# A two-layer diffusion step on one core: three quarters of a modulation vector move from TensorE to VectorE, and the table that spreads VectorE's dot products is given other shares

## The chip, the core and the metric

The kernel runs on one core of a Trainium2 chip. The metric is device time in microseconds (us): the median of three runs before is 2429.84 us (2428.86 to 2434.89). One further execution was profiled. Its parts are named as the profile names them: PE is TensorE's matmul row, PEld its weight loads, DVE is VectorE, ACT is ScalarE, POOL is GpSimd, SP is SyncE, which issues nearly all loads. "L415" is line 415 of the kernel before.

## The reference, cut to what matters

Two layers of a trunk are applied to 128 context tokens and 128 latent tokens of width 2048. The context tokens are modulated by `c_ctx`, the latent ones by `c`; otherwise they share all weights.

```
m = silu(cond) @ w_mod[l] + b_mod[l]          # cond: c_ctx, and c; six vectors of 2048
shift1, scale1, gate1, shift2, scale2, gate2 = split(m, 6)
q_r, k_r, v_r, g_r, q_a, k_a, v_a = split((rms(x) * (1 + scale1) + shift1) @ w_in[l])
x = x + gate1 * (concat(retention(...), attention(...)) @ w_out[l])
h = (rms(x) * (1 + scale2) + shift2) @ w_up[l]
x = x + gate2 * ((silu(gate) * val of a width-3 conv of h) @ w_down[l])
```

The six modulation vectors of a layer have the numbers 0 to 5 in this order. Vector 2, `gate1`, is the one that scales the output projection before it is added to `x`. All matrices are fp32 in memory; every weight is read once, 611.64 MB in all.

## The kernel before, in words

**The matmuls.** All tokens stand in the free dimension (256 columns). A big weight is cut into 128x128 tiles, and eight of them make a *piece* (512 KB, one DMA). There are 768 pieces in a fixed order: of layer 0 the heads (kv, q, ret; pieces 0 to 87), the output projection (88 to 119), then up and down projections in three thirds (120 to 383); of layer 1 kv and q (384 to 407), ret (408 to 471), out (472 to 503), up and down (504 to 767). Each weight is split into a rounded part `hi` (by ACT, L482) and the rest `lo` (by DVE, L483), and a tile takes three matmuls of 256 columns, hi by hi, hi by lo and lo by hi (L674 to L676). The splits run `LOOK` = 3 pieces ahead of PE: four pairs of buffers.

**The side tasks.** Attention and retention of a head are generators (`q_task`, `ret_task`); each piece ends with one step of the oldest one (a second step in mid-piece when two wait), so their small matmuls (L825 to L987, into PSUM tiles `aux`) stand between pieces, and their DVE and ACT parts stand in those engines' queues in the order of emission. No engine reorders its queue.

**The modulation vectors** are made in two ways. On PE: `emit_mod` and `emit_modq` multiply 32 columns of the condition by 128x512 tiles of `w_mod` (L406, L392); `emit_modq` makes a quarter of a vector (512 outputs) from four loads of 1 MB with four matmuls each, and `close_mod` copies the result on ACT, transposes it on PE (L447, four times) and reduces it on DVE. On DVE: `emit_dot` multiplies a row block of 128 outputs of `w_mod` by the broadcast condition and sums along the row (L415); a unit is one load of 1 MB and two such dot products, one for each condition. `DVESEQ` lists the vectors made this way, `PESEQ` and `QSEQ` those made on PE.

**Where they stand.** Before anything is emitted, `body` writes a list of events. PE's events follow `quota`, a line through the `knots`, in pairs: two loads' worth of matmuls after a piece. DVE's dot products follow `plan`: each has a due piece (six before the first use of its vector); `room` says how many dot products a piece may take in relation to others, from `DSHARE` by the kind of the piece, a fixed number in the heads of layer 0, and none from 6 pieces before to 12 behind the start of a norm (`QNORM`). A credit that grows with `room` times the rate still needed places them, mostly in twos on neighbouring pieces.

**The loads.** `pump` issues on SP's queue, in the order of the events, loads of modulation weights into `MODB` = 3 buffers `vec` and loads of pieces into `RAWB` = 5 buffers `raw`. A `vec` load is issued when the third-last user has released its buffer; SP waits at it, and what stands behind it in SP's queue waits too.

Of the kernel before, what the change touches and what calls it, by code (L numbers as in the profile page):

```python
# [48 lines left out]
def build_work():  # L49
# [51 lines left out]
    for it in items:  # L101
        g = groups[it["g"]]
        key = g["key"]
        for a in range(0, len(it["order"]), PIECE):
# [16 lines left out]
MU = KC * KC // MUNIT  # L121
# [2 lines left out]
PESEQ = [(0, 2), (0, 3)]  # L124

QSTART = [(0, 1 - i // 2, b) for b in range(4) for i in (0, 2)]
QMID = [(1, 2, 1), (1, 2, 2), (1, 2, 3)]
QNORM = {("up", 0): (0, 5, 0), ("kv", 1): (1, 2, 0), ("up", 1): (1, 5, 0)}
QSEQ = QSTART + QMID + list(QNORM.values())
DVESEQ = [(l, v, u) for l, v, n in ((0, 4, 0), (0, 5, 4), (1, 1, 0), (1, 0, 0), (1, 4, 0), (1, 3, 0), (1, 5, 4))  # L130
          for u in range(n, KC)]
DSHARE = {"kv": 0.38, "q": 0.38, "ret": 0.38, "out": 0.42, "up": 0.36, "down": 0.42}


@with_exitstack
def body(ctx: ExitStack, tc: tile.TileContext, io):
# [5 lines left out]
    mods = [("mod", (l, v, u)) for l, v in PESEQ for u in range(MU)]  # L142
    mods += [("modq", (*q, h)) for q in QMID for h in range(MU // 4)]
    dots = [(*d, k) for d in DVESEQ for k in range(2)]
    issued = [0, 0]
    gstart = {}
# [11 lines left out]
    def dot_event():  # L158

        if issued[1] < len(dots):  # L160
            l, v, u, k = dots[issued[1]]
            events.append(("dot", (l, v, u, k)))
            if (u, k) == (KC - 1, 1):
# [1 line left out]
            issued[1] += 1  # L165

    ahead = 3 * 2 * WIDE
    knots = [(ahead - 5, 0), (gstart["out", 0], 3 * MU // 2), (gstart["up", 0] - 6, 2 * MU), (gstart["kv", 1] + 16, 2 * MU),
             (gstart["out", 1] - 2, 11 * MU // 4)]

    def quota(j, knots):
        if j <= knots[0][0]:
# [9 lines left out]
    room = [0.0] * len(pieces)  # L182
    for j, p in enumerate(pieces):
        g = groups[p["it"]["g"]]
        ends = any(gstart[k] - 6 < j <= gstart[k] + 12 for k in QNORM)
        if not ends:
            if j >= gstart["out", 0]:
                room[j] = DSHARE[g["kind"]]
            elif j >= ahead or j >= 2 * WIDE and j % (2 * WIDE) >= 11:
                room[j] = 0.3  # L190
    plan, credit, nd = [0] * len(pieces), 0.0, 0
    for j in range(len(pieces)):
        while nd < len(dots) and due[nd] <= j:
# [25 lines left out]
    for j, p in enumerate(pieces):  # L219
        g = groups[p["it"]["g"]]  # L220
        kind, l = g["kind"], g["l"]
        if "gb" in p["it"] and p["first"]:
            w = 0 if kind == "kv" else 1
            start = j
            q = QNORM[kind, l]
# [20 lines left out]
        if j < 3 * nq:  # L246
            q, i = divmod(j, nq)
# [69 lines left out]
    def pump():  # L317

        while nload["mod"] < len(loads["mod"]) and held["mod"] < MODB:
# [3 lines left out]
            if key[0] == "dot":  # L323
                at = (DVESEQ.index(key[1]),)
            else:
# [94 lines left out]
    def end_dots(l, v):  # L420
        u = min(d[2] for d in DVESEQ if d[:2] == (l, v))
        dst = modT[l][:, v, u:, :]
        bias = C("bmod", l * 96 + v * KC + u, KC - u)
        nc.vector.tensor_tensor(dst, dst, bias.unsqueeze(2).to_broadcast([P, KC - u, 2]), op=ALU.add)
        if v in (1, 4):
            nc.vector.tensor_scalar_add(dst, dst, 1.0)
# [568 lines left out]
    with tc.manual_schedule():  # L995
# [13 lines left out]
        for ev, arg in events:  # L1009
# [31 lines left out]
            else:  # L1041
                j, hs = arg
# [12 lines left out]
def layout(inputs):  # L1055
# [21 lines left out]
    wm = a["w_mod"].reshape(DEPTH, D, 6, KC, P)  # L1077
    arrays["w_dot"] = np.stack([wm[l, :, v, u].T for l, v, u in DVESEQ])
    arrays["cb"] = np.ascontiguousarray(np.broadcast_to(np.stack([a["c_ctx"].reshape(D), a["c"].reshape(D)]), (P, 2, D)))
# [72 lines left out]
```

## Time and profile before

| | |
|---|---|
| median of three runs | 2429.84 us (2428.86 to 2434.89) |
| profiled execution: its own time, its span | 2432.38 us, 2430.6 us |
| PE busy, PEld busy | 2371.9 us (98%), 2204.5 us (91%) |
| DVE busy, ACT busy | 1892.6 us (78%), 1242.9 us (51%) |
| dot products on DVE (L415) | 208 of 2285 ns |
| splits on DVE (L483), on ACT (L482) | 768 of 1222 ns, 768 of 1051 ns |
| quarter matmuls on PE (L392), records | 448, of which 96 (three quarters) are touched |
| HBM read | 611.64 MB, 254 GB/s over the span |

A matmul's record is longer than the time to the next one, because they are pipelined; what one costs is read from start to start. The same holds, less so, for DVE. The 98% of PE is an average: it does not say how much of the span PE waits, which is read from the waits. The stretches of the program begin at these times in the trace: heads of layer 0 at 33.9 us, out at 388.7, up and down from 502.7, layer 1's kv and q at 1268.9, its ret pieces at 1343.6, its out at 1567.4, its up from 1669.3.

### The profile page before, as it was taken

What the parts mean: (1) busy time and instruction counts of PE and PEld (TensorE: products, weight loads), DVE (VectorE), ACT (ScalarE), POOL (GpSimd) and SP (SyncE); (2) the same over time, 40 slices, a digit from 0 to 9 for tenths busy, and PEclk for the clock granted to TensorE, in tenths of its full rate; (3) what the DMA queues carried; (4) which work ended last, traced back from release to release, by engine and by line L of the source; (5) the groups of instructions that cost most, each with busy time, mean ns of one, the idle gap of its engine ahead of it and who ended that gap; (6) DMA issues with size and microseconds to landing.
All of it is one profiled execution on the core that took longest, in us unless ns stands there. A gap on an engine that the chain in (4) does not pass through costs nothing.

```text
span 2430.6 us, 44608 instructions
## 1 busy us (share of the span) xinstructions
PE 2371.9 (98%) x18094; PEld 2204.5 (91%) x18094; DVE 1892.6 (78%) x2565; ACT 1242.9 (51%) x2005; POOL 27.5 (1%) x29
## 2 busy tenths in 40 slices
PE   6999999999999999999999999999999999999997
PEld 3888888899999999999989999999999888888886
DVE  4567777869998899889987787796997567666666
ACT  4534434465544555445556544456555555555555
POOL 0000010000000000000000000000000000000000
PEclk9999999999999999999999999999999999999999
DMA  9988788976787777777775687777675555655553
GB/s 382 351 310 325 277 301 321 354 261 240 282 283 272 252 275 254 275 271 252 264 281 192 245 290 280 289 275 257 231 245 188 190 186 182 190 190 186 190 181 122
DMA packets 146558, 619.27 MB, mean 255 GB/s; under 512 B 16304, under 2 KB 22448, under 8 KB 121392
## 3 DMA queue, kind: packets, MB, share of 16 engines
q1 hardware_dynamic: 138816, 605.24, 70.5%
q10 hardware_dynamic: 7536, 11.19, 1.3%
q8 instruction: 141, 2.31, 0.4%
q14 instruction: 65, 0.53, 0.1%
HBM read 611.64 MB, written 4.72 MB: 254 GB/s over the span
## 4 chain that ended last, share of the span: by engine, by line
PE 87%; DVE 6%; DMA 3%; issue 2%; ACT 2%; SPq 0%; DVEq 0%; POOLq 0%; ACTq 0%; POOL 0%
PE acc L674 20%; PE acc L676 19%; PE acc L675 19%; PE acc L614 15%; PE acc L616 8%; DVE lo L483 2%; PE md L392 2%; DVE hua L415 2%; DMA vec<-in_w_modq 1%; DMA vec<-in_w_mod 1%; PE md L406 1%; ACT hi L482 0%; ACT pr L874 0%; PE aux L902 0%; PE aux L447 0%
## 5 line engine op out<-in xcount | busy, mean ns | idle before, releaser
L483 DVE TENSOR_TENSOR lo<-raw,hi 128x1024 fp32r<-128x1024 f32 x768 | 934.4, 1222 | 245.2 <-ACT hi L482 241.3
L482 ACT CAST hi<-raw 128x1024 fp32r<-128x1024 f32 x768 | 804.0, 1051 | 476.7 <-PE acc L675 354.8
L674 PE MATMUL acc<-hT,hi 128*128 128x256 f32 x3328 | 950.5, 286 | 5.9 <-ACT hT L577 5.9
L676 PE MATMUL acc<-hT,lo 128*128 128x256 f32 x3328 | 931.3, 280 | 2.0 <-DVE lo L483 2.0
L675 PE MATMUL acc<-hT,hi 128*128 128x256 f32 x3328 | 931.8, 280 | 0.6 <-DVE hT L582 0.6
L674 PEld LDWEIGHTS acc<-hT,hi 128*128 128x128 f32 x3328 | 626.9, 188 | 35.4 <-issue 17.0
L675 PEld LDWEIGHTS acc<-hT,hi 128*128 128x128 f32 x3328 | 625.8, 188 | 4.5 <-issue 1.9
L676 PEld LDWEIGHTS acc<-hT,lo 128*128 128x128 f32 x3328 | 627.0, 188 | 3.0 <-DVE lo L483 2.8
L415 DVE SCALAR_TENSOR_TENSOR hua<-vec,cbc 128x2048 bf16<-128x2048 f32 x208 | 475.2, 2285 | 0.7 <-DMA vec<-in_w_dot 0.7
L676 PE MATMUL acc<-ypair,lo 128*128 128x256 f32 x1216 | 344.3, 283 | 2.3 <-DVE lo L483 2.3
L674 PE MATMUL acc<-ypair,hi 128*128 128x256 f32 x1216 | 346.0, 285 | 0.0
L675 PE MATMUL acc<-ypair,hi 128*128 128x256 f32 x1216 | 344.0, 283 | 0.0
L614 PE MATMUL acc<-hT,hi 128*128 128x512 f32 x896 | 316.7, 396 | 0.0
L616 PE MATMUL acc<-hT,lo 128*128 128x256 f32 x896 | 252.7, 282 | 0.0
L614 PE MATMUL acc<-ypair,hi 128*128 128x512 f32 x704 | 247.2, 396 | 0.0
L674 PEld LDWEIGHTS acc<-ypair,hi 128*128 128x128 f32 x1216 | 233.2, 192 | 6.8 <-issue 5.0
L676 PEld LDWEIGHTS acc<-ypair,lo 128*128 128x128 f32 x1216 | 233.2, 192 | 3.0 <-DVE lo L483 3.0
L675 PEld LDWEIGHTS acc<-ypair,hi 128*128 128x128 f32 x1216 | 233.3, 192 | 0.1
L614 PEld LDWEIGHTS acc<-hT,hi 128*128 128x128 f32 x896 | 168.4, 188 | 40.6
L616 PE MATMUL acc<-ypair,lo 128*128 128x256 f32 x704 | 197.5, 281 | 0.0
L616 PEld LDWEIGHTS acc<-hT,lo 128*128 128x128 f32 x896 | 168.3, 188 | 0.0
L614 PEld LDWEIGHTS acc<-ypair,hi 128*128 128x128 f32 x704 | 132.1, 188 | 31.5
(145 smaller groups left out, 1584.2 us busy)
## 6 DMA issues: line engine op xcount, KB each, us to landing
raw<-in_w_up SPq DMA_DIRECT2D x352, 512.0 KB, 4.4
vec<-in_w_dot SPq DMA_DIRECT2D x104, 1024.0 KB, 5.2
raw<-in_w_in SPq DMA_DIRECT2D x176, 512.0 KB, 5.4
raw<-in_w_down SPq DMA_DIRECT2D x176, 512.0 KB, 4.2
vec<-in_w_modq SPq DMA_DIRECT2D x56, 1024.0 KB, 7.2
vec<-in_w_mod SPq DMA_DIRECT2D x32, 1024.0 KB, 8.0
raw<-in_w_out SPq DMA_DIRECT2D x64, 512.0 KB, 5.5
xT<-in_xT ACTq DMA_DIRECT2D x2, 1024.0 KB, 9.9
```

Source lines behind the costliest of these rows:

```text
L392: nc.tensor.matmul(md[0][32 * j:32 * j + 32, :], sc[:, 2 * kc:2 * kc + 32], t[:, 512 * i:512 * i + 512], start=kc < 4, stop=kc >= 12)
L406: nc.tensor.matmul(md[0][32 * j:32 * j + 32, :], sc[:, 2 * u:2 * u + 32], t[:, 512 * j:512 * j + 512], start=u == 0, stop=u == MU - 1)
L415: nc.vector.scalar_tensor_tensor(hua.rearrange("p c t -> p (c t)").bitcast(BF16), raw[key], 1.0, acc[:, k, :], op0=ALU.mult, op1=ALU.mult, ...
L482: nc.scalar.copy(hi, r)
L483: nc.vector.tensor_tensor(lo, r, hi.bitcast(F32), op=ALU.subtract)
L614: nc.tensor.matmul(out, hi_t[j][:, P * i:P * i + P], src, start=c[n] == 1, stop=False, skip_group_check=True)
L616: nc.tensor.matmul(out[:, 0:256], lo_t[j][:, P * i:P * i + P], src[:, 0:256], start=False, stop=c[n] == nk, skip_group_check=True)
L674: nc.tensor.matmul(out, hi, src[:, 0:256], start=first, stop=False, skip_group_check=True)
L675: nc.tensor.matmul(out, hi, src[:, 256:512], start=False, stop=False, skip_group_check=True)
L676: nc.tensor.matmul(out, lo, src[:, 0:256], start=False, stop=last, skip_group_check=True)
```

## The change

`QMID` held quarters 1, 2 and 3 of layer 1's vector 2; they are taken from PE, and the 12 units of 128 outputs that they made are put into `DVESEQ` between vectors 0 and 4 of layer 1. Quarter 0 stays on PE, in the norm at the start of layer 1. The two knots that spread the PE events over layer 1's heads go. And `DSHARE` and the number for the heads of layer 0 are changed, which moves dot products of all vectors.

```
--- before.py
+++ after.py
@@ -124,12 +124,12 @@
 PESEQ = [(0, 2), (0, 3)]
 
 QSTART = [(0, 1 - i // 2, b) for b in range(4) for i in (0, 2)]
-QMID = [(1, 2, 1), (1, 2, 2), (1, 2, 3)]
+QMID = []
 QNORM = {("up", 0): (0, 5, 0), ("kv", 1): (1, 2, 0), ("up", 1): (1, 5, 0)}
 QSEQ = QSTART + QMID + list(QNORM.values())
-DVESEQ = [(l, v, u) for l, v, n in ((0, 4, 0), (0, 5, 4), (1, 1, 0), (1, 0, 0), (1, 4, 0), (1, 3, 0), (1, 5, 4))
+DVESEQ = [(l, v, u) for l, v, n in ((0, 4, 0), (0, 5, 4), (1, 1, 0), (1, 0, 0), (1, 2, 4), (1, 4, 0), (1, 3, 0), (1, 5, 4))
           for u in range(n, KC)]
-DSHARE = {"kv": 0.38, "q": 0.38, "ret": 0.38, "out": 0.42, "up": 0.36, "down": 0.42}
+DSHARE = {"kv": 0.5, "q": 0.5, "ret": 0.5, "out": 0.5, "up": 0.32, "down": 0.42}
 
 
 @with_exitstack
@@ -165,8 +165,7 @@
             issued[1] += 1
 
     ahead = 3 * 2 * WIDE
-    knots = [(ahead - 5, 0), (gstart["out", 0], 3 * MU // 2), (gstart["up", 0] - 6, 2 * MU), (gstart["kv", 1] + 16, 2 * MU),
-             (gstart["out", 1] - 2, 11 * MU // 4)]
+    knots = [(ahead - 5, 0), (gstart["out", 0], 3 * MU // 2), (gstart["up", 0] - 6, 2 * MU)]
 
     def quota(j, knots):
         if j <= knots[0][0]:
@@ -187,7 +186,7 @@
             if j >= gstart["out", 0]:
                 room[j] = DSHARE[g["kind"]]
             elif j >= ahead or j >= 2 * WIDE and j % (2 * WIDE) >= 11:
-                room[j] = 0.3
+                room[j] = 0.4
     plan, credit, nd = [0] * len(pieces), 0.0, 0
     for j in range(len(pieces)):
         while nd < len(dots) and due[nd] <= j:
```

With 232 dot products for 208 the plan comes out so (dot products by stretch, before and now; PE's pairs are where they were but for those taken out):

| pieces | before | now |
|---|---|---|
| 24 to 87, heads of layer 0 | 20 | 24 |
| 88 to 119, out of layer 0 | 14 | 18 |
| 120 to 183, first up | 24 | 20 |
| 184 to 383, the rest of layer 0 | 86 | 88 |
| 384 to 407, kv and q of layer 1 | 5 | 7 |
| 408 to 471, ret of layer 1 | 27 | 40 |
| 472 to 503, out of layer 1 | 14 | 17 |
| 504 to 567, up of layer 1 | 18 | 18 |

From line 169 on, a line of the changed kernel has a number lower by one. Three places follow.

DVE in the second attention task of layer 1, around pieces 412 to 416 (`lo` is the split of a piece, `hua` a dot product, `st` and `pr` are the softmax's, `modT` on L424 and L426 the bias of a finished vector), before:

```order
L483 TENSOR_TENSOR lo<-raw,hi 128x1024
L880 TENSOR_TENSOR st<-st 128x4
L881 RECIPROCAL st<-st 128x4
L882 TENSOR_TENSOR pr<-pr,st 128x512
L415 SCALAR_TENSOR_TENSOR hua,modT<-vec,cbc 128x2048
L424 TENSOR_TENSOR modT<-modT,cst 128x32
L426 TENSOR_SCALAR modT<-modT 128x32
L483 TENSOR_TENSOR lo<-raw,hi 128x1024
L880 TENSOR_TENSOR st<-st 128x2
L881 RECIPROCAL st<-st 128x2
L882 TENSOR_TENSOR pr<-pr,st 128x512
L483 TENSOR_TENSOR lo<-raw,hi 128x1024 x2
```

and now:

```order
L482 TENSOR_TENSOR lo<-raw,hi 128x1024
L879 TENSOR_TENSOR st<-st 128x4
L880 RECIPROCAL st<-st 128x4
L881 TENSOR_TENSOR pr<-pr,st 128x512
L414 SCALAR_TENSOR_TENSOR hua,modT<-vec,cbc 128x2048
L482 TENSOR_TENSOR lo<-raw,hi 128x1024
L879 TENSOR_TENSOR st<-st 128x2
L880 RECIPROCAL st<-st 128x2
L881 TENSOR_TENSOR pr<-pr,st 128x512
L414 SCALAR_TENSOR_TENSOR hua,modT<-vec,cbc 128x2048
L482 TENSOR_TENSOR lo<-raw,hi 128x1024 x2
L865 TENSOR_REDUCE st<-aux 128x2
```

A dot product stands now behind each of the two normalisations, where before the second had none behind it.

DVE in a retention task of layer 1, the head whose first step is at piece 440 (`bs`, `ag` and `grs` are the group norm's statistics, `ro` its result, `ry` and `ypair` the gated output), before:

```order
L975 BN_STATS bs<-ro 128x6 x2
L977 BN_AGGR ag<-bs 128x2 x2
L978 TENSOR_SCALAR grs<-ag 128x2
L483 TENSOR_TENSOR lo<-raw,hi 128x1024
L982 TENSOR_SCALAR ro<-ro,ag,grs 128x128 x2
L483 TENSOR_TENSOR lo<-raw,hi 128x1024
L989 SCALAR_TENSOR_TENSOR ry<-aux,cst,grp 128x256
L799 TENSOR_TENSOR ypair<-ry,ypair 128x256
L415 SCALAR_TENSOR_TENSOR hua,modT<-vec,cbc 128x2048
L483 TENSOR_TENSOR lo<-raw,hi 128x1024
L415 SCALAR_TENSOR_TENSOR hua,modT<-vec,cbc 128x2048
```

and now:

```order
L974 BN_STATS bs<-ro 128x6 x2
L976 BN_AGGR ag<-bs 128x2 x2
L977 TENSOR_SCALAR grs<-ag 128x2
L414 SCALAR_TENSOR_TENSOR hua,modT<-vec,cbc 128x2048
L482 TENSOR_TENSOR lo<-raw,hi 128x1024
L981 TENSOR_SCALAR ro<-ro,ag,grs 128x128 x2
L414 SCALAR_TENSOR_TENSOR hua,modT<-vec,cbc 128x2048
L482 TENSOR_TENSOR lo<-raw,hi 128x1024
L988 SCALAR_TENSOR_TENSOR ry<-aux,cst,grp 128x256
L798 TENSOR_TENSOR ypair<-ry,ypair 128x256
L482 TENSOR_TENSOR lo<-raw,hi 128x1024
L414 SCALAR_TENSOR_TENSOR hua,modT<-vec,cbc 128x2048
```

Where a head's eight pieces held two to four dot products, they hold five.

SP's queue in the output projection of layer 0, up to the load of the first part of the norm's quarter (`in_w_modq`), before:

```order
L329 DMA vec<-in_w_dot 128x2048
L329 DMA vec<-in_w_mod 128x2048 x2
L339 DMA raw<-in_w_out 128x1024 x4
L329 DMA vec<-in_w_dot 128x2048
L339 DMA raw<-in_w_out 128x1024 x3
L329 DMA vec<-in_w_dot 128x2048
L329 DMA vec<-in_w_mod 128x2048
L339 DMA raw<-in_w_out 128x1024
L329 DMA vec<-in_w_mod 128x2048
L339 DMA raw<-in_w_out 128x1024 x2
L339 DMA raw<-in_w_up 128x1024
L329 DMA vec<-in_w_modq 128x2048
```

and now:

```order
L328 DMA vec<-in_w_dot 128x2048 x2
L328 DMA vec<-in_w_mod 128x2048
L338 DMA raw<-in_w_out 128x1024 x4
L328 DMA vec<-in_w_mod 128x2048
L338 DMA raw<-in_w_out 128x1024 x3
L328 DMA vec<-in_w_dot 128x2048 x2
L328 DMA vec<-in_w_mod 128x2048
L338 DMA raw<-in_w_out 128x1024 x3
L328 DMA vec<-in_w_mod 128x2048
L338 DMA raw<-in_w_up 128x1024 x3
L328 DMA vec<-in_w_modq 128x2048 x3
```

The first load of the norm's quarter, which followed a dot product's release, now stands behind the second load of the last pair of `in_w_mod`, and is released by the first matmuls of that pair.

## Rows read from the trace of the kernel before

**Rows 1.** The page: busy time by engine, and the chain that ended last.

```profile
PE 2371.9 (98%) x18094; PEld 2204.5 (91%) x18094; DVE 1892.6 (78%) x2565; ACT 1242.9 (51%) x2005; POOL 27.5 (1%) x29
...
PE 87%; DVE 6%; DMA 3%; issue 2%; ACT 2%; SPq 0%; DVEq 0%; POOLq 0%; ACTq 0%; POOL 0%
```

**Rows 2.** Windows: stretch, us, busy of each engine, clock, DMA share, GB/s.

```profile
33.90:388.70 354.80, 338.59 (x2711) 292.89 (x2712) 243.97 (x399) 158.58 (x259) 8.66 (x7) 0.99 0.84 321
388.70:502.70 114.00, 111.56 (x915) 99.24 (x913) 87.88 (x111) 51.21 (x90) 1.38 (x2) 1.00 0.90 346
780.40:961.30 180.90, 180.90 (x1538) 180.90 (x1537) 167.73 (x209) 92.25 (x127) 0.00 (x0) 1.00 0.74 260
...
1440.00:1560.00 120.00, 119.45 (x996) 113.98 (x996) 93.86 (x138) 50.98 (x74) 7.26 (x5) 1.00 0.79 283
```

**Rows 3.** PE in order of time around a pair: start us, us, instruction.

```profile
1446.24 0.28 PE L676 MATMUL acc<-hT,lo 128*128 128x256 f32 x1
1446.45 1.92 PE L392 MATMUL md<-vec,sc 128*32 128x512 f32 x16
1448.30 0.39 PE L674 MATMUL acc<-hT,hi 128*128 128x256 f32 x1
1448.53 0.28 PE L675 MATMUL acc<-hT,hi 128*128 128x256 f32 x1
```

**Rows 4.** PE in order of time around a quarter's transposes.

```profile
1566.89 0.28 PE L676 MATMUL acc<-hT,lo 128*128 128x256 f32 x1
1567.02 0.60 PE L447 MATMUL aux<-cst,mev 128*128 128x128 f32 x4
1567.37 0.36 PE L674 MATMUL acc<-ypair,hi 128*128 128x256 f32 x1
```

**Rows 5.** DVE in order of time in a retention head of layer 1.

```profile
1463.96 2.28 DVE L415 SCALAR_TENSOR_TENSOR hua<-vec,cbc 128x2048 bf16<-128x2048 f32 x1
...
1466.17 1.22 DVE L483 TENSOR_TENSOR lo<-raw,hi 128x1024 fp32r<-128x1024 f32 x1
```

**Rows 6.** The same window's dot products (L415) alone: busy us, records.

```profile
1440.00:1560.00 120.00, 35.40 (x31) 1.00 0.79 283
```

**Rows 7.** Chain of waits in layer 1's second attention task: start, us, what.

```profile
1375.36 2.38 DVE lo L483 x2
1377.73 0.61 DVE st L866
...
1379.97 0.66 PE aux L889 x4
```

**Rows 8.** Chain of waits in out of layer 0, piece 101.

```profile
430.20 7.62 DMA vec<-in_w_mod
```

**Rows 9.** SP and PE at the norm's quarter of layer 0.

```profile
478.30 0.33 SPq L329 DMA_DIRECT2D vec<-in_w_modq  x1
478.51 1.92 PE L406 MATMUL md<-vec,sc 128*32 128x512 f32 x16
483.87 1.07 PE L392 MATMUL md<-vec,sc 128*32 128x512 f32 x8
```

**Rows 10.** Line L329, all loads of modulation weights.

```profile
DMA to landing us min/median/max: 4.7/6.4/14.0
```

**Rows 11.** Chain of waits in the heads of layer 0, piece 51.

```profile
211.13 0.57 DVE hua L415
...
215.36 10.16 DMA vec<-in_w_mod
```

**Rows 12.** PE's waits from 208.5 to 388.7 us: total, times, longest.

```profile
PE aux L968 <- DVE rk L954: 2.8, 3, 2.0
PE aux L889 <- ACT pr L874: 2.7, 3, 1.5
PE md L406 <- DMA vec<-in_w_mod: 2.4, 2, 1.6
```

**Rows 13.** PE's waits from 560 to 576 us, in the first up.

```profile
PE acc L676 <- DVE lo L483: 1.6, 2, 0.9
```

More of the change, by code (lines that the diff above doesn't have):

```diff
@@ L126 @@
 QSTART = [(0, 1 - i // 2, b) for b in range(4) for i in (0, 2)]
-QMID = [(1, 2, 1), (1, 2, 2), (1, 2, 3)]
+QMID = []
 QNORM = {("up", 0): (0, 5, 0), ("kv", 1): (1, 2, 0), ("up", 1): (1, 5, 0)}
 QSEQ = QSTART + QMID + list(QNORM.values())
-DVESEQ = [(l, v, u) for l, v, n in ((0, 4, 0), (0, 5, 4), (1, 1, 0), (1, 0, 0), (1, 4, 0), (1, 3, 0), (1, 5, 4))
+DVESEQ = [(l, v, u) for l, v, n in ((0, 4, 0), (0, 5, 4), (1, 1, 0), (1, 0, 0), (1, 2, 4), (1, 4, 0), (1, 3, 0), (1, 5, 4))
           for u in range(n, KC)]
-DSHARE = {"kv": 0.38, "q": 0.38, "ret": 0.38, "out": 0.42, "up": 0.36, "down": 0.42}
+DSHARE = {"kv": 0.5, "q": 0.5, "ret": 0.5, "out": 0.5, "up": 0.32, "down": 0.42}
 @with_exitstack
@@ L167, in body @@
     ahead = 3 * 2 * WIDE
-    knots = [(ahead - 5, 0), (gstart["out", 0], 3 * MU // 2), (gstart["up", 0] - 6, 2 * MU), (gstart["kv", 1] + 16, 2 * MU),
-             (gstart["out", 1] - 2, 11 * MU // 4)]
+    knots = [(ahead - 5, 0), (gstart["out", 0], 3 * MU // 2), (gstart["up", 0] - 6, 2 * MU)]
     def quota(j, knots):
@@ L189, in body @@
             elif j >= ahead or j >= 2 * WIDE and j % (2 * WIDE) >= 11:
-                room[j] = 0.3
+                room[j] = 0.4
     plan, credit, nd = [0] * len(pieces), 0.0, 0
```

## The prediction

> **What bounds the kernel now.** I read the page first. PE is busy 98% of the span, and the chain that ended last lies on PE for 87%, on DVE for 6% and on loads for 3% [rows 1]: work taken off PE shortens the span, unless another engine or a load is late where it was. DVE's 78% is a mean, so I read stretches next [rows 2]. In an up stretch of layer 0 DVE is busy 167.73 of 180.90 us (93%) and PE all of it, so 93% alone makes no wait there. In the heads of layer 0 PE is idle for 16.2 of 354.8 us, in the out projection of layer 0 for 2.4 of 114.0, in layer 1's ret pieces (window 1440 to 1560) for 0.6 of 120. Third, the chain and the waits inside the stretches, to see what ended PE's idle time: side tasks that pass through DVE, and loads into the three `vec` buffers [rows 7, 8, 11, 12]. The sum is made against the profiled execution, 2432.38 us; it stands 2.5 us above the median of 2429.84, and I carry the difference over unchanged.
>
> **1. PE's work that goes.** Six pairs of two loads (eight matmuls each) and three closings. From the matmul before a pair to the one behind it are 1448.30 − 1446.24 = 2.06 us [rows 3], where an ordinary step is 1567.02 − 1566.89 = 0.13 [rows 4], 0.12 as a mean of neighbouring ones; and the matmul behind the pair is 0.23 from the next instead of 0.12. A pair thus costs 2.06 − 0.12 + 0.11 = 2.05, six cost 12.3. A closing's four transposes cost 1567.37 − 1566.89 − 0.12 = 0.36 [rows 4], three cost 1.1. Sum: **−13.4**. ACT's copies and DVE's reductions of the closings go too; I count them at nothing, since they lie beside PE's work. The bytes loaded stay the same.
>
> **2. Attention of layer 1 (pieces 400 to 419).** Here the chain goes from PE through DVE and back: two splits from 1375.36, the softmax's `st` (L866) at 1377.73, then L889 on PE at 1379.97 [rows 7]. In the changed queue twelve dot products stand in these pieces for eight, one behind each normalisation (the first place shown of the order). A dot product takes 2.21 us from its start to the next one's, 1466.17 − 1463.96 [rows 5]. Walking DVE's queue with such durations, each instruction starting when its predecessor is done and its input there, DVE's idle time takes in most of the 8.8 us, and L866 comes at about 1378.1, 0.4 later. PE, 2.05 earlier by the pair taken out at 412, waits for it: **+2.5**. Bounds: 0, if the idle time takes in all and lets the chain move up; 4.7, if one dot product more (2.21) stands uncovered.
>
> **3. Ret pieces of layer 1.** In the window of 120 us DVE is busy 93.86 [rows 2], and dot products are 35.40 of it, 31 records or 15.5 dot products, two records each [rows 6]. From start to start they hold 15.5 × 2.21 = 34.3, so the rest is 59.6. Now 40 stand where 27 stood: 15.5 × 40/27 = 23.0 in the same pieces, and DVE has 59.6 + 23.0 × 2.21 = 110.4 us to do. PE needs 120 less three pairs and a closing, 113.5. That is 97%, above any stretch in the trace, but there is cover: the head's side tasks have a step per piece, and a split runs three pieces ahead. I take **0**. Bounds: −0.8 (PE's 0.6 of idle time and some go), and +4.4, the rate at which dot products cost PE in layer 0's heads (0.34 each, step 5) for the 13 added.
>
> **4. Out of layer 0.** A `vec` load starts when the third-last user has released its buffer. Before, one pair's second load was issued three pieces ahead of its use; the chain runs through it, 430.20 with 7.62 to landing [rows 8], so PE waited for it, and the lead is at most 7.6. Now there are four such pairs, by the order; with the median landing of 6.4 us [rows 10] none of the new three is late, with 7.62 each is a little: I take +0.7 for the three. Then the norm's quarter. Its first load was issued at 478.30 behind a dot product, and its matmuls started at 483.87 [rows 9]. Now the first half of the last pair releases it (the third place of the order): that pair starts at 478.51 and takes 1.92, its half is done at 479.47, and 4.4 us remain. With the median landing PE waits 2.0. Sum **+2.7**; with the shortest landing, 4.7, it is 1.0, and with the 10.16 of another load of such a pair [rows 11] 6.5.
>
> **5. Heads of layer 0.** The wait for `w_mod` at piece 51 was begun by a dot product: SP issued that load at 215.36 because a release by a dot product (211.13) came late [rows 11]. These dot products move two pieces forward and the wait of 2.4 [rows 12] goes: **−2.4**, or 0 if another load takes its place. Against that stand four more dot products between the tasks' chains. PE waits there 2.8 + 2.7 us for `rk` and `pr` [rows 12] with some 16 dot products in the stretch, 0.34 each; four more cost **+1.4**. Bounds: 0, and 4.4, half of their own time.
>
> **6. First up of layer 0 (pieces 120 to 183).** 20 dot products for 24: PE's waits for `lo`, 1.6 us [rows 13], go: **−1.6**, at worst 0.
>
> **7. The rest.** Last third of layer 0 and out of layer 1 take five more, at the DVE load that made no wait in the up stretch [rows 2], and the out of layer 1 has its own releases changed: **+0.5**, between −1 and +2.
>
> Sum: −13.4 + 2.5 + 0 + 2.7 − 2.4 + 1.4 − 1.6 + 0.5 = **−10.3**: 2422.1 profiled, **2419.6** as a median. All bounds at their best make −18.2, at their worst +8.6.
>
> **Rivals.** A: DVE absorbs everything. Steps 2, 4, 5's addition and 7 cost nothing, −13.4 − 2.4 − 1.6 = −17.4, 2412.4. For it speaks the up stretch with 93% and no wait; against it that in layer 1's attention the chain already passes through DVE [rows 7], and that the release of the norm's quarter is later by the order itself. The Trainium skill ("Perfetto Trace Analysis", Identifying the Most-Contended Engine) would judge so: it takes occupancy as a fair measure for VectorE, judges TensorE by weight-load occupancy, and has the engine with the higher one optimized first; by 91% against 78% that is TensorE, and the time would be rival A's. The trace agrees for the up stretch and not for the attention.
>
> B: VectorE's side chains eat the gain. Steps 2, 3 and 5 at their upper bounds are 2.2 + 4.4 + 3.0 = 9.6 more: 2429.2. For it: 97% in the ret pieces is beyond what the trace shows, and a side task's step that is late by one dot product is seen by PE at its next step. Against it: in the window of before, at 78%, PE was idle for only 0.6 [rows 2].
>
> C, slower than before: the loads of the modulation weights come too late in out of layer 0. Three new pairs have at most 7.6 us from issue to use, the quarter 4.4. If such a load takes x us there, PE waits 3(x − 7.6) + (x − 4.4) = 4x − 27.2. From x = 10.1 on, 13.0 are lost instead of 2.7 and the kernel is slower than before; at 12 it is 20.8, or 2437.7. For it: landings up to 14.0 [rows 10], and the highest DMA share of the stretches here, 0.90 [rows 2]. Against it: the median of 6.4.
>
> D: the change does not do what it says. The order shows L392 and L447 gone from the ret pieces and the dot products in place, so this has next to no chance; it would leave 2430.
>
> **How the numbers follow.** Forecast (2416 to 2424) 0.42, A 0.18, B 0.28, C 0.10, D 0.02. A measurement of this kernel tells some 0.3%, 7.3 us, from no change: faster is below 2422.5, slower above 2437.1. Of the forecast's 0.42 some 0.34 lies below 2422.5, and with A's 0.18 faster has 0.52. Slower is most of C and a tail of B, 0.08; the rest, 0.40, is the same. The range of 2412 to 2433 leaves out half of A below and most of C above. The forecast's own range is 2416 to 2424.
>
> **What would show it.** Step 1: in the ret pieces L392 and L447 are gone, and the stretch, 1343.6 to 1567.4 before, is some 10 us shorter; it is wrong if it shortens by less than 6, and then DVE's busy share there above 95% with PE's `aux` waits on DVE speaks for B. Step 2: L866 around piece 416 is later against PE, with a wait of 2 to 3 us. Step 4: the out stretch, 114.0, is 2 to 3 longer, with PE's waits for L392's and L406's loads; over 120 is C. Step 5: the heads of layer 0, 354.8, about a microsecond shorter, with no wait of 2.4 for a load. Step 6: the first up stretch loses its 1.6. The prediction as a whole is wrong if layer 0 together is longer by more than 4 us, or if ret of layer 1 keeps its length.

## The result: slower by 0.7%, and the profile after

The changed kernel takes 2450.63 us (median of five runs, 2445.92 to 2453.55) beside 2434.01 us for the kernel before in the same comparison: a ratio of 1.0072, 95% interval 1.0053 to 1.009. The prediction said 2419.6 us, faster, within 2412 to 2433. It was wrong in sign and size. The profiled execution has a span of 2448.8 us against 2430.6, 18.2 more.

The page of the changed kernel, busy time by engine and the chain that ended last:

```profile
PE 2362.0 (96%) x17986; PEld 2203.7 (90%) x17986; DVE 1940.2 (79%) x2608; ACT 1243.3 (51%) x2002; POOL 31.1 (1%) x29
...
PE 83%; DVE 9%; DMA 3%; issue 2%; ACT 2%; SPq 0%; DVEq 0%; ACTq 0%; POOLq 0%; POOL 0%
```

PE is busy for 9.9 us less than before and DVE for 47.6 more [rows 1]; PE's share of the chain went from 87% to 83%, DVE's from 6% to 9%. PE now waits where it did not. Where, the windows by stretch show (columns as in [rows 2]). Of the kernel before, pieces 48 to 87 (heads of layer 0), 400 to 431 (the attention tasks of layer 1) and 432 to 471 (its other ret pieces):

```profile
208.50:388.70 180.20, 168.94 (x1331) 145.74 (x1328) 141.15 (x251) 73.98 (x143) 8.66 (x7) 1.00 0.81 304
1315.80:1433.00 117.20, 114.91 (x921) 107.97 (x920) 96.15 (x151) 56.00 (x106) 5.26 (x2) 1.00 0.70 250
1433.00:1567.40 134.40, 133.85 (x1120) 126.82 (x1118) 103.57 (x147) 56.54 (x83) 7.26 (x5) 1.00 0.78 280
```

Of the changed kernel, the same three, and in second place the out projection of layer 0 (114.00 in [rows 2]):

```profile
209.30:398.90 189.60, 169.94 (x1331) 146.26 (x1328) 148.92 (x257) 77.90 (x150) 8.65 (x7) 1.00 0.80 304
398.90:519.70 120.80, 113.36 (x916) 100.07 (x914) 94.32 (x118) 51.24 (x90) 3.29 (x2) 0.99 0.89 338
1334.70:1463.00 128.30, 114.50 (x885) 109.98 (x884) 106.53 (x157) 55.30 (x105) 3.36 (x2) 0.96 0.61 215
1463.00:1587.50 124.50, 124.50 (x1046) 123.97 (x1046) 118.34 (x163) 55.22 (x80) 9.91 (x5) 1.00 0.80 282
```

The differences in the profiled executions are +9.4, +6.8, +11.1 and −9.9 us; 2.2 more come in the last down stretch of layer 0, 1.6 behind layer 1's norm, −1.8 in the first up, −1.8 from the up stretch of layer 1 to the end, and +0.8 before piece 48. The −1.8 at the end holds −3.5 from the last 200 pieces, where the kernels do not differ; without it the change costs 21.7 us in the traces. The last two of the four rows should be read together. Where DVE is busiest (118.34 of 124.50, 95%) PE waits for nothing; where DVE is busy 83% of the time (106.53 of 128.30) PE is idle for 13.8 us. PE's waits name who ended them (total, times, longest). The kernel before, pieces 48 to 87, beside the waits for `rk` and `pr` of [rows 12], and then pieces 400 to 431:

```profile
PE aux L987 <- ACT ra L945: 1.5, 2, 1.4
PE aux L889 <- DVE pr L882: 0.6, 1, 0.6
...
PE aux L902 <- ACT pt L891: 1.0, 1, 1.0
PE aux L987 <- ACT ra L945: 0.8, 1, 0.8
PE aux L889 <- ACT pr L874: 0.6, 1, 0.6
```

The changed kernel, pieces 48 to 87:

```profile
PE aux L986 <- ACT ra L944: 5.5, 4, 1.4
PE aux L967 <- DVE rk L953: 5.2, 4, 1.6
PE aux L888 <- ACT pr L873: 3.1, 2, 2.9
PE aux L888 <- DVE pr L881: 1.5, 2, 0.9
```

And pieces 400 to 431:

```profile
PE aux L888 <- ACT pr L873: 8.8, 2, 5.8
PE aux L986 <- ACT ra L944: 3.0, 1, 3.0
PE aux L967 <- DVE rk L953: 1.6, 1, 1.6
PE aux L901 <- ACT pt L890: 0.4, 1, 0.4
```

All are matmuls of side tasks that need a step of DVE or ACT. In pieces 48 to 87 these waits grew from 7.6 us to 15.3, in pieces 400 to 431 from 2.4 to 13.8. What stands behind the longest is in the chain of waits at piece 416 (start, us, what):

```profile
1397.27 0.86 PE aux L859 x4
...
1399.40 2.29 DVE hua L414 x2
1401.69 2.27 DVE lo L482 x2
1403.97 0.61 DVE st L865
1404.60 0.17 DVE st L866
...
1405.13 1.03 ACT pr L873 x4
...
1406.21 1.11 PE aux L888 x4
```

It is the chain of [rows 7] with a dot product (`hua`) ahead of it: two splits that had been waiting behind the dot product, the softmax's `st`, ACT's exponentials, and only then PE, after 5.8 us of waiting. In [rows 7] two splits and `st` came without one directly ahead. The scores that `st` needs (L859 on PE) were ready at 1398.13, and DVE came to them 5.8 us later; in the kernel before (L860, from 1376.11 for 1.03) 0.6 us later.

The third loss is a load. The chain at the norm's quarter of layer 0, changed kernel:

```profile
488.56 2.21 DVE hua L414 x2
490.77 1.15 DVE lo L482
...
491.94 0.33 SPq L338
...
492.36 6.79 DMA vec<-in_w_modq
...
499.29 1.70 PE md L391 x8
```

SP stood at the load of a piece (L338), whose buffer a split frees, and that split stood behind a dot product. The quarter's load came behind it in the queue, 492.36. PE waited for it alone:

```profile
PE md L391 <- DMA vec<-in_w_modq: 4.1, 1, 4.1
```

### The profile page after: what moved, and what is told of

Same layout as the page of the kernel before. It is cut to its first block, busy times and chain, and to the rows that moved or that the text cites. A ratio compares the mean times of both kernels' runs of the same rounds, so it can differ in the third digit from the quotient of the medians.

```text
span 2448.8 us, 44457 instructions
## 1 busy us (share of the span) xinstructions
PE 2362.0 (96%) x17986; PEld 2203.7 (90%) x17986; DVE 1940.2 (79%) x2608; ACT 1243.3 (51%) x2002; POOL 31.1 (1%) x29
## 4 chain that ended last, share of the span: by engine, by line
PE 83%; DVE 9%; DMA 3%; issue 2%; ACT 2%; SPq 0%; DVEq 0%; ACTq 0%; POOLq 0%; POOL 0%
PE acc L673 19%; PE acc L675 19%; PE acc L674 18%; PE acc L613 15%; PE acc L615 8%; DVE hua L414 3%; DVE lo L482 3%; DMA vec<-in_w_modq 2%; PE md L391 1%; DMA vec<-in_w_mod 1%; PE md L405 1%; DMA raw<-in_w_in 0%; ACT hi L481 0%; PE aux L901 0%; ACT pr L873 0%
## 5 line engine op out<-in xcount | busy, mean ns | idle before, releaser
L414 DVE SCALAR_TENSOR_TENSOR hua<-vec,cbc 128x2048 bf16<-128x2048 f32 x232 | 530.0, 2285 | 2.0 <-DMA vec<-in_w_dot 2.0
```

Source lines behind the costliest of these rows:

```text
L414: nc.vector.scalar_tensor_tensor(hua.rearrange("p c t -> p (c t)").bitcast(BF16), raw[key], 1.0, acc[:, k, :], op0=ALU.mult, op1=ALU.mult, ...
```

## The experiments

Totals are medians and ratios against the kernel before on the same chip; a ratio is taken over all runs, so it is not quite that of the two medians, and versions on different chips are compared by their ratios (1.0072, 1.0053 to 1.009, for the changed kernel). Stretches come from one profile each. Profiles with the same dot products and pairs in a stretch differ there by up to 0.6 us in pieces 400 to 431, 1.7 in pieces 48 to 87, 2.2 in the first up and 2.6 in out of layer 0. The last 200 pieces, where no dot product stands, took 575 us in some profiles and 578.7 in others, so totals of single profiles are not compared.

**1. The shares alone, and the quarters alone.** Kernel before with the new shares:

```
-DSHARE = {"kv": 0.38, "q": 0.38, "ret": 0.38, "out": 0.42, "up": 0.36, "down": 0.42}
+DSHARE = {"kv": 0.5, "q": 0.5, "ret": 0.5, "out": 0.5, "up": 0.32, "down": 0.42}
-                room[j] = 0.3
+                room[j] = 0.4
```

> The kernel before with only the new shares (DSHARE, and 0.4 in the heads of layer 0): the quarters stay on TensorE, 208 dot products, 24 of them in the heads of layer 0, 16 in out, 36 in layer 1's ret pieces. Theory 1 (the place of the dot products costs: each that stands directly ahead of a step of a side task on VectorE makes TensorE wait): +15 to +22 us against before, with the heads of layer 0 about +9, out +3 to +6, ret pieces +6 to +10 longer. Theory 2 (the cost is in having 24 dot products more, not in the shares): 0 to +4 us. Theory 3 (the pairs on TensorE only filled time in which it would have waited for side tasks): as theory 1 in the heads and out, but the ret pieces no longer than before, since their pairs are still there as filling: +9 to +14 us.

Measured: 2457.31 against 2429.66 us, 1.0113 (1.0099 to 1.0128). The shares alone lose 27.6 us, more than the whole change: pieces 48 to 87 +13.5, out +7.3, pieces 400 to 431 +6.8, pieces 432 to 471 +0.8. Theory 2 falls; theory 1 has the sign and too small a size; theory 3 wanted about half of it or less.

The changed kernel with the old shares (the same edit, the other way round, on the changed kernel):

> The changed kernel with the old shares: the quarters leave TensorE, 232 dot products, heads and out of layer 0 as before (20 and 14), ret pieces of layer 1 with 32 for 27, the other new ones beside up and down of layer 0. Theory 1: -4 to -10 us against before. Theory 2: +10 to +17, as the changed kernel. Theory 3: 0 to +5 us.

Measured: 2430.26 against 2429.66 us, 1.0003 (0.9994 to 1.0012): no change. Theory 1 wanted −4 to −10, theory 2 +10 to +17; theory 3's 0 to +5 holds for the total. Pieces 48 to 87 are 2.1 longer, out is as before; pieces 432 to 471 are 9.8 shorter, pieces 400 to 431, with 16 dot products for 14, 4.9 longer, the last down stretch of layer 0 3.2 longer. Beside the −10.2 of experiment 2, this is what 24 more dot products cost under the old shares.

**2. Is PE's work worth its time?** Three quarters left out, dot products as before (the two knots of layer 1's heads go as in the change):

```
-QMID = [(1, 2, 1), (1, 2, 2), (1, 2, 3)]
+QMID = []
...
+    nc.vector.memset(modT[1][:, 2, 4:, :], 1.0)
```

> Three quarters of layer 1's vector 2 are left out altogether (their places hold ones); the dot products stand as before, old shares. Theory 1 and 2: TensorE's 13.4 us come off nearly whole, -10 to -14 us against before. Theory 3: the waits for side tasks grow by as much as the pairs took, -4 to 0 us, with the ret pieces of layer 1 shorter by less than 4.

Measured: 2419.49 against 2429.66 us, 0.9953 (0.9939 to 0.9966), −10.2. Its windows for pieces 400 to 431 and 432 to 471:

```profile
1315.60:1432.60 117.00, 112.12 (x885) 108.08 (x884) 96.19 (x149) 55.27 (x105) 5.25 (x2) 0.99 0.61 213
1432.60:1557.60 125.00, 124.45 (x1048) 123.70 (x1047) 102.48 (x145) 55.06 (x80) 7.26 (x5) 1.00 0.72 245
```

The second is 9.4 shorter than before, as four pairs should make it. The first is 0.2 shorter though two pairs and a closing (4.5 us) are gone: PE's wait for `pr` there grew from 0.6 to 3.1, and the same 885 matmuls keep PE busy for 112.12 us, where a version without that wait has 110.23 (the last of experiment 6): behind the wait they run at a lower granted clock, 0.99 as a mean for 1.00. Theory 3 is wrong for the whole and right beside the attention tasks: those two pairs filled a wait. (The version also loads 12 MB less; PE had no wait for a load in these pieces before.)

**3. The heads of layer 0.** Changed kernel with `room[j] = 0.3` there:

> The changed kernel with 0.3 instead of 0.4 in the heads of layer 0 (20 dot products there instead of 24, the others in the up and down stretches); all else as changed. Theory 1: -8 to -10 us against the changed kernel, all of it in the heads of layer 0, which are as long as before (354.8). Theory 2: 0 to -3. Theory 3 says nothing of it.

Measured: 2445.89 against 2429.66 us, 1.0066 (1.0051 to 1.008). Beside the changed kernel's 1.0072 that is no difference clear of the noise, where theory 1 wanted −8 to −10. Its windows for pieces 48 to 87 and out:

```profile
211.00:389.80 178.80, 168.94 (x1331) 146.08 (x1328) 141.20 (x251) 73.74 (x143) 10.62 (x7) 1.00 0.83 306
389.80:514.40 124.60, 113.86 (x916) 100.48 (x914) 95.91 (x120) 51.16 (x90) 1.38 (x2) 0.96 0.90 334
```

The heads give back all, 189.6 to 178.8. But out, with the same eighteen dot products on other pieces, grows from 120.8 to 124.6, and the norm's quarter is later still:

```profile
PE md L391 <- DMA vec<-in_w_modq: 7.8, 1, 7.8
```

Is it the number of dot products or the piece? The kernel before, those of the heads one piece later:

```
+    plan[24:89] = map(int, "00000011000000000000001100011000110001100011000110001100011000011")
```

> The kernel before with the dot products of the heads of layer 0 one piece later each, as many as before (20). Theory P: the heads of layer 0 change by several us, 3 to 12, most likely longer; theory N: they stay within 1 us of 354.8.

Measured: 2432.18 against 2432.12 us, 0.9998 (0.9985 to 1.0011): nothing in the total, a miss for theory P as it was put. Pieces 48 to 87, with one of their sixteen pushed out to piece 88, took 184.1 us for 180.2, and groups of eight pieces moved by between −1.6 and +3.1, so the piece does matter, but the differences nearly cancel. And the price of the sixteen that stood there: the kernel before with those cut to 64 of 2048 columns:

```
+        n = 64 if (l, v) == (0, 4) and 2 <= u < 10 else 2048
```

> The kernel before in which the sixteen dot products of pieces 50 to 87, in the heads of layer 0, work on 64 of their 2048 columns (so a part of layer 0's vector 4 is left uncomputed); loads, order and releases are the same. Constant price (the 9.2 us for four more dot products hold for each, 2.2 us or its whole length): the stretch of 354.8 us loses all that TensorE waits there for side tasks, 8 us or more. Rising price (the first ones lie in VectorE's idle time, only the last cost): it loses 2 to 4 us.

Measured: 2426.35 against 2430.72 us, 0.9979 (0.997 to 0.9988). The window for pieces 48 to 87:

```profile
209.80:385.90 176.10, 169.92 (x1331) 146.62 (x1328) 110.73 (x252) 73.86 (x143) 4.84 (x7) 0.99 0.84 311
```

That is 4.1 us less than before for 30 us of DVE's work taken away: 0.26 for each of the sixteen. (The expectation named the whole heads stretch; it begins with the start-up, whose time differs between profiles by up to 5 us, so pieces 48 to 87 are taken.) The changed kernel's four more cost 9.4, 2.35 each as a mean, a dot product's whole length (2.21 in [rows 5]). The constant price falls. That the number makes the price rise is likely, but no run isolates it, since 0.4 for 0.3 also moves the others: sixteen at three sets of places took 178.8 to 182.3 us, fifteen 184.1, twenty at two sets 189.6 and 193.7. So the places alone are worth some 4 us, and twenty took longer at both of theirs.

**4. Out of layer 0.** Changed kernel with PE's last pairs four pieces earlier, all dot products in place:

```
-(gstart["up", 0] - 6, 2 * MU)]
+(gstart["up", 0] - 10, 2 * MU)]
```

> The changed kernel with one knot moved by four pieces, so that TensorE's last pairs in out of layer 0 stand earlier (the last at piece 110 instead of 114); the dot products stand as changed, 18 in out. Theory L (out of layer 0 lost its time to loads that were issued late): PE's waits for loads of 4.1 and 1.7 us there go, and the stretch is 5 to 7 us shorter than in the changed kernel. Rival D (VectorE's four more dot products cost it): no change, within 1 us.

Measured: 2440.33 against 2432.12 us, 1.0036 (1.0022 to 1.0049) beside 1.0072, some 9 us below the changed kernel. Its window for out:

```profile
398.50:511.30 112.80, 111.27 (x915) 99.30 (x913) 93.96 (x117) 51.10 (x90) 3.29 (x2) 1.00 0.94 362
```

8.0 us shorter with the same eighteen dot products, and no wait of PE for a load is left there. Theory L holds, and the rival as it was put falls. Dot products still have a part in it: the chain above runs through one, and the same eighteen on other pieces made the wait 7.8 (experiment 3).

**5. The attention tasks of layer 1.** Changed kernel with thirteen dot products of pieces 404 to 427 moved away:

```
...
+    plan[400:432] = map(int, "11100000000000000000111100001111")
```
(Nine of them went into pieces 216 to 279 and 312 to 359, four to pieces 402, 422, 428 and 431.)

> The changed kernel with its 232 dot products, but none between pieces 403 and 419 and at 424 to 427 of layer 1: thirteen of the attention tasks' 22 places are emptied, four of them filled again behind the chains (402, 422, 428, 431) and nine moved into up stretches of layer 0; heads and out of layer 0 as in the changed kernel. Theory P (what costs is the piece at which a dot product stands ahead of a step of a side task, not how many there are): pieces 400 to 431 go from 128 to about 113 us, -12 to -16 us against the changed kernel. Theory N (each dot product beside heads costs some 0.4 us wherever it stands): -3 to -4 us.

Measured: 2448.58 against 2432.12 us, 1.0064 (1.0045 to 1.0083), beside 1.0072 no difference clear of the noise. The windows, pieces 400 to 431 and then the last down stretch of layer 0:

```profile
1343.80:1461.90 118.10, 112.37 (x885) 108.71 (x884) 85.66 (x137) 55.37 (x105) 3.35 (x2) 0.97 0.57 189
1202.80:1294.90 92.10, 80.63 (x620) 74.31 (x618) 75.42 (x116) 42.95 (x80) 0.69 (x1) 0.92 0.74 255
```

The attention pieces give back 10.2 us, two thirds of the 15 that theory P wanted, with nine dot products fewer. The down stretch takes 92.1 where the changed kernel took 81.9, and gives it away again. Nine is odd: from there on the two dot products of one load stand in different pairs of pieces, a half-used load holds one of the three `vec` buffers through the norm, and the norm's quarter is loaded late:

```profile
PE md L394 <- DMA vec<-in_w_modq: 5.0, 1, 5.0
```

That the parity does it is read from the order of releases and this wait, not tried by itself.

**6. Chosen places.** All 232 dot products, at pieces chosen from the tables above: heads and out of layer 0 as before, 114 in pieces 120 to 359, ten in pieces 400 to 431.

```
...
+    plan[400:432] = map(int, "00110000000000000000111000111110")
...
```

> The changed kernel with its 232 dot products at chosen pieces: heads and out of layer 0 as in the kernel before, more of them beside up and down of layer 0 (114 in pieces 120 to 359 for 98), ten in pieces 400 to 431 of layer 1 at places behind the chains of the attention tasks, five per head in the pieces after that as in the changed kernel. Theory P: the 13.4 us of TensorE come off and no wait replaces them: -10 to -16 us against the kernel before (some 2418). Theory N: 33 dot products in the ret pieces for 27 and 24 more in all cost 0.4 each as in the run with the quarters alone: 0 to -4 us.

Measured: 2423.78 against 2432.12 us, 0.9965 (0.9951 to 0.9979), −8.3: faster than both kernels, by less than theory P wanted. Pieces 400 to 431 take 116.0 us, with PE busy in 111.5 of them. Two of the three dot products at 420 to 422 moved into layer 1's up stretch:

> The version with chosen places, with two of its three dot products at pieces 420 to 422 of layer 1 moved to the up stretch of layer 1 (24 there for 22), both units whole on either side. Theory P: the last attention chain, pieces 424 and 425, loses 2 to 4 us of wait, the kernel is 2 to 4 us faster than with the chosen places, 10 to 14 below the kernel before. Theory N: under 1 us.

Measured: 2423.07 against 2430.72 us, 0.9968 (0.9956 to 0.998): the total is as with the chosen places, as theory N wanted. Pieces 400 to 431 gain 3.6 (112.4 us), as theory P wanted, but the up stretch with 24 dot products loses 4.4 (188.4), with waits of 3.5 us for `lo`. And with the same number in every stretch, at pieces 411, 412 and 431 instead of 420 to 422:

> The version with chosen places with three of the ten dot products of pieces 400 to 431 in layer 1 at other pieces (411, 412 and 431 instead of 420 to 422): the same number in every stretch. Theory P (place): pieces 400 to 431, 116 us with the chosen places, are 3 to 4 us shorter (112 to 113) and the kernel is as much faster, 10 to 14 below the kernel before. Theory N (number): no change, within 1 us.

Measured: 2421.17 against 2431.87 us, 0.9948 (0.993 to 0.9967), −10.7. The window for pieces 400 to 431:

```profile
1317.90:1429.70 111.80, 110.23 (x885) 106.46 (x884) 82.68 (x134) 55.27 (x105) 1.38 (x2) 1.00 0.57 188
```

4.2 shorter than with the chosen places by moving three of ten (2.2 of it come back in the pieces behind, 127.8 for 125.6). Here the piece decides. Of all versions this one has the lowest ratio, though its interval overlaps those of the other two; its −10.7 are the 13.4 us of step 1 less 2.7.

## Why the prediction was wrong, step by step

| step | forecast | profile | |
|---|---|---|---|
| 1, 3: pieces 432 to 471, four pairs and two closings | −8.9 | −9.9 | right: 95% of DVE without a wait |
| 1, 2: pieces 400 to 431, two pairs and a closing | −2.0 | +11.1 | wrong |
| 4: out of layer 0 | +2.7 | +6.8 | mechanism right, size short |
| 5: heads of layer 0 | −1.0 | +9.4 (+0.8 more before piece 48) | wrong |
| 6: first up of layer 0 | −1.6 | −1.8 | right in kind, the size partly luck |
| 7: the rest | +0.5 | +2.7 | +6.2 but for the last 200 pieces |

- **Step 2 failed first.** It walked DVE's queue with PE's emission as it was and found DVE's idle time to take in the dot products but for 0.4 us. In the trace no idle time lies where it was needed: the last before the wait at piece 416 are 2.1 us that end at 1392.9, and from there to 1405 DVE works without a break. The dot product behind the normalisation and the two splits behind it stand ahead of `st`, whose input was ready at 1398.13, before that dot product began. The waits for `pr`, `ra` and `rk` there are 13.4 us, where before they were 1.4. A second term is the granted clock, which the sum had at nothing: the same 885 matmuls keep PE busy for 114.50 us at 0.96, and for 110.23 at 1.00 in the last version of experiment 6, so by estimate some 4.3 us go to it. And of the 4.5 us that step 1 took off here for two pairs and a closing, experiment 2 got 0.2.
- **Step 5 failed as much.** It priced four more dot products at the mean of those that stood there, 0.34 each. The mean was about right (0.26 by the short ones), and the four more, with the places that came with them, cost 2.35 each. The upper bound, half of a dot product's own time, was itself too low; nothing in the trace excluded the whole of it. The wait of 2.4 us at piece 51 did go down, to 1.2, not to 0 as step 5 counted it, and [rows 11] were read too short: between the dot product's release and the load the chain of the kernel before has a split and SP's load of a piece.

```profile
211.13 0.57 DVE hua L415
211.70 1.56 issue
213.34 1.15 DVE lo L483
214.51 0.33 SPq L339
214.93 0.38 SPq L329
```

- **Step 4** had the right load and release. It left out SP's queue, which these rows already show: the first half of the last pair (488.73, 1.06 long) had freed the buffer, and the load was issued 2.6 us later, because loads of pieces stood ahead of it, so PE waited 4.1 us where 2.0 were predicted. About 1.7 us more went to the granted clock behind that wait (last section), again a term at nothing in the sum. Moving the pair removes the wait (experiment 4).
- **Step 6** has the mechanism: PE's waits for `lo` in the first up fell from 1.6 to 0.4 us. That the stretch agrees to 0.2 is luck: with all 24 dot products and the same waits of 1.6, the version of experiment 2 was 1.5 us shorter there too.
- **Step 1** is right where PE is bound: experiment 2 gives 10.2 of 13.4. Rival B named two of the places and the kind of loss, but put 9.6 us on it; against the forecast the attention pieces lost 13.1 and the heads 10.4, and the pieces behind, where B wanted 4.4, lost nothing. Rival C's stretch, out of layer 0, has 4.1 more than the forecast, but the quarter's load took 6.79 us to land, not C's 10.1: it was issued late. Of the prediction's own signs of being wrong the first came, layer 0 is 16.3 us longer, and the second nearly: ret of layer 1 is only 2.0 shorter, 221.8 for 223.8.
- The Trainium skill ("Perfetto Trace Analysis", Identifying the Most-Contended Engine) has the engine with the higher occupancy optimized first, by weight loads PE at 91% before DVE at 78%. The trace agrees that PE's work is worth taking off, 10.2 us in experiment 2. Rival A's 2412 needed more, that DVE takes the work in for nothing, and there the trace differs: at 83% in pieces 400 to 431 its place in a chain decided, and at 95% in the pieces behind it lost nothing.

## What to carry to other kernels

The busy share of an engine that serves dependent chains says little about what one more piece of filler costs: look at what stands right ahead of the chain's next step in its in-order queue, and price an added instruction there at up to its whole length, not at the mean of those already placed. A long wait also costs granted clock behind it, here by estimate 4.3 us in the attention pieces. A load's lead is counted to the moment its queue can issue it, past the loads that stand before it, not to the moment its buffer is free. Work on a bound engine is worth its time only in stretches where that engine does not wait.

## What the runs showed of the hardware

The changed kernel's waits of 5.8 and 4.1 us cost more than their length. Behind the 5.8 us at piece 416 the matmuls start 0.21 us apart instead of 0.12, and the granted clock is half, 1.2 of 2.4 GHz, for the next microseconds. The changed kernel in windows: the wait, what follows, and later; then out of layer 0 behind the wait for the norm's quarter; then the kernel before behind the wait of [rows 7] (columns as above, the granted clock third from the end):

```profile
1398.00:1406.20 8.20, 2.40 (x15) 1.71 (x13) 6.90 (x12) 1.21 (x6) 0.00 (x0) 0.87 0.62 208
1407.30:1409.90 2.60, 2.60 (x14) 2.60 (x13) 2.52 (x5) 1.53 (x2) 0.00 (x0) 0.50 0.46 184
...
1414.00:1418.00 4.00, 4.00 (x34) 3.89 (x33) 2.34 (x5) 2.24 (x3) 0.00 (x0) 1.00 0.78 270
...
499.20:503.00 3.80, 3.71 (x17) 2.27 (x18) 0.00 (x0) 0.00 (x0) 0.00 (x0) 0.55 0.99 412
...
1379.90:1384.00 4.10, 4.03 (x31) 3.93 (x32) 3.28 (x6) 2.46 (x6) 0.00 (x0) 1.00 0.56 219
```

By these rows, as an estimate, 1.3 us are lost in 2.6 us at half clock and about 1.7 in 3.8 us at 0.55, on top of the waits of 5.8 and 4.1. Behind the wait of [rows 7], 0.6 us long, the clock stayed at 1.00.
